# One layer of a hybrid decoder on one core: norm sums with split operands, the new tokens' matmuls placed in rows with other visits, and two down products that take their last k-tile at their end

## The chip, the cores and the metric

The kernel runs on one core of a Trainium2 chip. Its time is the device time of one execution in microseconds (us), and a kernel's time is the median of several runs. A core has a matrix engine (TensorE, PE in the profile; its weight loads are PEld), a vector engine (VectorE, DVE), an activation engine (ScalarE, ACT), a general engine (GpSimd, POOL) and a queue engine that starts most transfers (SyncE, SP). Each works through its own list of instructions in order and waits on semaphores for the others.

## The reference

One inference step of one layer for 256 prompt tokens and 8 x 4 = 32 sample tokens that share all weights (288 columns, T in the kernel), with model width 2048 and feed-forward width 5632, all in float32:

```python
z = x @ w_in                                # h, gate_b, gate_c, q, k, v, g_a, g_b
ya = gate_b * causal_dwconv3(gate_c * h)
yb = merged dilated window attention of q, k, v  (3 groups x 4 heads of 128; the sample
     tokens attend to cached keys and values and to their own new ones)
mixed = sigmoid(g_a) * (ya @ w_branch_a) + sigmoid(g_b) * (yb @ w_branch_b)
x1 = layernorm(ALPHA * x + mixed @ w_out) * ln1_g + ln1_b
a, b = split(x1 @ w_up)
y  = layernorm(ALPHA * x1 + (silu(causal_dwconv3(a)) * b) @ w_down) * ln2_g + ln2_b
```

The caches and the last rows of the convolutions are returned too.

## The kernel before

**Products.** Activations lie with the features on the 128 partitions and the 288 tokens in the columns. Each weight block is 128 output features by up to 16 k-tiles of 128. To keep float32 accuracy with the faster matmul type fp32r, both operands are split into a high part (rounded to fp32r) and a low part (the rest): `split` does it for activations, with a copy on ACT (L214) and a subtraction on DVE (L215). `prepare` (L162) loads the next weight block into `wst` (three buffers, L167) and `half_block` splits it by halves of eight k-tiles into `whi` on ACT (L138) and `wlo` on DVE (L139), four buffers each. `product` (L187) takes one prepared block, asks for the next to be prepared, and `mms` (L202) issues three matmuls for each k-tile into one PSUM accumulator `acc` (five buffers): high by high (L208), high weights by low activations (L209), low weights by high activations (L210). A full product is 48 matmuls. The program goes from one `product` to the next: q; k and v with the prompt's attention between; the convolution mixer; the gates with `w_a` and `w_b`; `w_out`; then the feed-forward part in three parts (`THIRDS`, 16, 16 and 12 tiles of 128), each with its up products (L726 and L739) and sixteen down products (L756).

**Order.** The program is written for a tile framework that adds the semaphores and orders each engine's list itself, by a model of the timeline, within the dependencies; the order written in the source is therefore not the order on an engine. `behind` and `in_a_row` (L301) force a given order on PE where they are used.

**Sample attention.** `sample_steps` (L392) is a generator that `product` advances every five or so products. A step is one visit of PE: plain float32 matmuls of 32 output rows for each head against cache tiles, tied together by `in_a_row`. Scores are L407, the values L460. The softmax lies between them (L428 to L434), then the transposes of the probabilities (L437, L439) and of the new values (L447). DVE masks the operands of a visit by batch (L369). The scores of the new tokens against each other are twelve small matmuls at L424, issued in the step after the last score visit; the new tokens' part of the values are four matmuls at L471, after the first value visit. `fetch_two` loads the next two cache tiles through SP and stores them to the output.

**Norms.** `Norm` (L600) keeps, for each of two layer norms, the running sums of the deviations and of their squares over 16 feature tiles. `first` takes the mean over partitions of the first tile as an offset with one float32 matmul against `ones_p` (L610). `add` adds each tile to the sums on POOL (L622, L623); the last tile is not added there: the sums and the last tile each go through a float32 matmul against `ones_d` (L630, L631), four in all. `finish` makes mean and 1/std for the first norm (L636), `finish_out` the end of the kernel (L650). The first norm's result is not applied before the up products of part one: they run on scaled but unnormalised tiles, and `normed` (L709) corrects each result with 1/std (L714, L715).

**Part one of the feed-forward.** Its gated tiles are split into `yah`/`yal` (here `gh`, `gl`), one k-tile after the other; the down products read all sixteen. Meanwhile POOL and ACT turn `dd` into the normalised tile (L750 to L752), which is split into `xh`/`xl` for the later parts (L758).

Of the kernel before, what the change touches and what calls it, by code (L numbers as in the profile page):

```python
# [11 lines left out]
F32R = mybir.dt.float32r  # L12
# [5 lines left out]
P = 128  # L18
# [65 lines left out]
def layer_kernel(ctx: ExitStack, tc: tile.TileContext, ins, outs):  # L84
# [14 lines left out]
    def sb(pl, shape, tag, dt=F32, bufs=None):  # L99
        return pl.tile(shape, dt, tag=tag, name=nm(tag), bufs=bufs)  # L100

    def acc(half=H):
        return sb(ps, [P, half, 2], "acc")
# [4 lines left out]
    def h3(ap):  # L108
        return ap.rearrange("p k (h a) -> p k h a", h=2)

    def att(cols=512):
        return sb(ps, [P, cols], "att", bufs=2)

    def f32(ap):
        return ap.bitcast(F32)
# [68 lines left out]
                if prompt[1] is None:  # L184
                    prompt[0] = None

    def product(x):  # L187

        w = w_ready.pop(0)
        if not w_ready:  # L190
            prepare()
        if steps_on[0]:
            spent[0] += N_STEP
            while spent[0] >= N_STEP_BLOCKS:
                spent[0] -= N_STEP_BLOCKS
                next(steps, None)
        o = acc(x[0].shape[-1])
        mms(o, w, x)
        prompt_step()
        return o.rearrange("p a h -> p h a")  # L200

    def mms(out, w, x):  # L202
        nk = sum(n for _, _, n in w)
        k = 0
        for hi, lo, n in w:
            for c in range(n):
                xh_k, xl_k = (t[:, k].rearrange("p h a -> p a h") for t in x)
                pe.matmul(out, hi[:, c, :], xh_k, start=k == 0, stop=False)  # L208
                pe.matmul(out, hi[:, c, :], xl_k, start=False, stop=False)  # L209
                last_mm[0] = pe.matmul(out, lo[:, c, :], xh_k, start=False, stop=k == nk - 1)  # L210
                k += 1

    def split(hi, lo, src):
        act.copy(hi, src)  # L214
        dve.tensor_tensor(lo, src, f32(hi), ALU.subtract)  # L215

    ones_d = sb(big, [P, P], "ones_d")
    ones_p = sb(big, [P, P], "ones_p")
    pool.memset(ones_d, 1.0 / D)
    pool.memset(ones_p, 1.0 / P)  # L220


    zero = sb(wk, [P, T], "cy", F32R, bufs=2)
# [168 lines left out]
    def sample_steps():  # L392
        fetch_two()
        yield
        row = []
        s = sw2[:, :SW]
        sbias = cst[:, C_SB : C_SB + SW]
        for g in range(NG):
            qm = by_batch(q_s[:, g])
            cols = P if g == 0 else NT * P  # L400
            p = sb(ps, [P, cols], "long", bufs=1)
            for b in range(NB):
                if g > 0 or b % 4 == 0:
                    c = cache_tiles.pop(0)
                o = (b % 4) * NH * P if g == 0 else 0
                for j in range(NH):
                    row.append(pe.matmul(  # L407
                        p[j * NS : (j + 1) * NS], qm[:, j, b, :], c[:, o + j * cols : o + (j + 1) * cols],
                        start=b == 0, stop=b == NB - 1,
                    ))  # L410
                if b == NB - 1 or (g > 0 and b % 2 == 1):
                    in_a_row(row)
                    row = []
                    fetch_two()
                    yield
            sg = s[:, g * P : (g + 1) * P]
            if g == 0:
                dve.tensor_tensor(sg, p, sbias[:, :P], ALU.add)
            else:
                pick_t(sg, p, sbias[:, g * P : (g + 1) * P])  # L420
        pn = sb(ps, [P, NG * NS], "long", bufs=1)
        for j in range(NH):
            for g in range(NG):
                pe.matmul(  # L424
                    pn[j * NS : (j + 1) * NS, g * NS : (g + 1) * NS], q_s[:, g, j, :], k_s[:, g, j, :],
                    start=True, stop=True,
                )
        dve.tensor_tensor(s[:, NG * P :], pn, sbias[:, NG * P :], ALU.add)  # L428
        st = sb(wk, [P, 4], "st", bufs=4)
        dve.reduce_max(st[:, 0:1], s, AX.X)  # L430
        dve.tensor_scalar_mul(st[:, 1:2], st[:, 0:1], -SCALE)
        act.activation(s, s, AF.Exp, bias=st[:, 1:2], scale=SCALE, accum_out=st[:, 2:3])
        dve.reciprocal(st[:, 3:4], st[:, 2:3])
        dve.tensor_scalar_mul(s, s, st[:, 3:4])  # L434
        pt = att()
        for g in range(NG):
            pe.transpose(pt[:, g * P : (g + 1) * P], s[:, g * P : (g + 1) * P], ident)  # L437
        pt2 = att()
        pe.transpose(pt2[: NG * NS, :P], s[:, NG * P :], ident)  # L439
        sT = sw2[:, : NG * P].rearrange("p (g r) -> p g r", g=NG)  # L440
        act.copy(sT, pt[:, : NG * P].rearrange("p (g r) -> p g r", g=NG))
        sTn = sw2[: NG * NS, NG * P : NG * P + P]
        act.copy(sTn, pt2[: NG * NS, :P])
        vn = sw2[: NG * NS, NG * P + P : NG * P + P + NH * P].rearrange("p (j d) -> p j d", j=NH)
        pv = att()
        for j in range(NH):
            pe.transpose(pv[: NG * NS, j * P : (j + 1) * P], v_s[:, j].rearrange("p g r -> p (g r)"), ident)  # L447
        act.copy(vn, pv[: NG * NS].rearrange("p (j d) -> p j d", j=NH))
        o_sb = sw2[:, NG * P + P + NH * P : NG * P + 2 * P + NH * P]
        for g in range(NG):  # L450
            sm = by_batch(sT[:, g].rearrange("p (j r) -> p j r", j=NH))
            cols = P if g == 0 else NT * P
            if g < 2:
                p = sb(ps, [P, cols], "long", bufs=1)
            for b in range(NB):
                if g > 0 or b % 4 == 0:
                    c = cache_tiles.pop(0)
                o = (b % 4) * NH * P if g == 0 else 0
                for j in range(NH):
                    row.append(pe.matmul(  # L460
                        p[j * NS : (j + 1) * NS], sm[:, j, b, :], c[:, o + j * cols : o + (j + 1) * cols],
                        start=b == 0 and g < 2, stop=b == NB - 1 and g == 2,
                    ))
                if b == NB - 1 or (g > 0 and b % 2 == 1):
                    in_a_row(row)
                    row = []
                    fetch_two()
                    yield
            if g == 0:
                for j in range(NH):  # L470
                    pe.matmul(  # L471
                        p[j * NS : (j + 1) * NS], sTn[:, j * NS : (j + 1) * NS], vn[:, j, :], start=False, stop=True
                    )
                act.copy(o_sb, p)
            elif g == 2:
                pick_t(o_sb, p, o_sb)
        po = att(P)
        pe.transpose(po, o_sb, ident)
        oT = sw[:, :P]
        act.copy(oT, po)  # L480
        split(ybh[:, :, SEQ:], ybl[:, :, SEQ:], oT.rearrange("p (j r) -> p j r", j=NH))
        yield
# [117 lines left out]
    class Norm:  # L600


        def __init__(self, g, b):
            self.g, self.b = g, b
            self.s1, self.s2, self.c = (lw[:, k] for k in range(3))

        def first(self):

            p = att(T)
            pe.matmul(p, ones_p, dd[:, 0], start=True, stop=True)  # L610
            act.copy(self.c, p)
            dve.tensor_tensor(dd[:, 0], dd[:, 0], self.c, ALU.subtract)

        def add(self, i):
            d = dd[:, i]
            last = i == KD - 1
            q = self.s2 if i == 0 else sb(wk, [P, T], "cy", bufs=2)
            act.activation(q, d, AF.Square)
            if i == 0:
                pool.tensor_copy(self.s1, d)  # L620
            elif not last:
                pool.tensor_tensor(self.s1, self.s1, d, ALU.add)  # L622
                pool.tensor_tensor(self.s2, self.s2, q, ALU.add)  # L623
            if i == KD - 2:

                act.activation(lw[:, 3, 0:1], q[:, 0:1], AF.Abs_reciprocal_sqrt)
            if last:
                self.p1, self.p2 = att(T), att(T)
                for p, s, e in ((self.p1, self.s1, d), (self.p2, self.s2, q)):
                    pe.matmul(p, ones_d, s, start=True, stop=False)  # L630
                    pe.matmul(p, ones_d, e, start=False, stop=True)  # L631

        def at(self, c, i):
            return prm[:, c + i : c + i + 1]
# [51 lines left out]
                sp.dma_start(out[:, k0 : k0 + n, :], y[:, k0 : k0 + n, :])  # L686


    n1 = Norm(R_LN, R_LN + KD)
    for i in range(KD):  # L690
        o = product((h3(mxh), h3(mxl)))
        xf = sb(wk, [P, T], "h", bufs=2)
# [25 lines left out]

    cf = sb(big, [P, KF, 2 + 2 * NB], "qk_s")
    f = 0  # L720
    n2 = Norm(R_LN + 2 * KD, R_LN + 3 * KD)
    for part, nf in enumerate(THIRDS):
        gh = sb(big, [P, KD, T], "yah", F32R)
        gl = sb(big, [P, KD, T], "yal", F32R)
# [27 lines left out]
                act.activation(dd[:, k], dd[:, k], AF.Identity, bias=n1.at(n1.b, k), scale=n1.at(n1.g, k))  # L752
        if f == KF:
            sp.dma_start(outs["o_cf"].rearrange("p (k r) -> p k r", k=KF), cf)
        for i in range(KD):
            o = product((h3(gh), h3(gl)))  # L756
            if part == 0:
                split(x[0][:, i], x[1][:, i], h2(dd[:, i]))  # L758
                dve.scalar_tensor_tensor(h2(dd[:, i]), h2(dd[:, i]), ALPHA, o, ALU.mult, ALU.add)
# [194 lines left out]
```

## Time and profile before

| | |
|---|---|
| median of 3 runs | 1764.37 us (1764.05 to 1764.5) |
| the profiled execution's own time | 1764.45 us |
| its span (first to last instruction of the profile) | 1762.7 us |
| busy: PE / PEld / DVE / ACT / POOL | 1744.4 / 1713.7 / 1008.0 / 797.3 / 254.1 us |
| mean granted clock of PE | 0.997 |
| DMA | 436.25 MB, mean 247 GB/s |
| matmuls of `product`, by line L208 / L209 / L210 | 4512 each, about 0.286 us from start to end of one |
| plain float32 records of the norms, L610 / L630 / L631 | 4 / 8 / 8, 0.406 us each |
| records L424 / L471 | 24 / 8, 0.200 / 0.285 us each |

A plain float32 matmul shows as two records. Matmuls are pipelined, so the time that one takes of PE is read from the distance between starts, not from its duration. A line number in the profile is a line of the kernel before, and the same work has other numbers in the changed kernel.

### The profile page before, as it was taken

To read this page: it belongs to the slowest core of one execution; us is meant where nothing else is said; L and a number is where in the kernel's file an instruction comes from. 1 tells how busy PE (TensorE), PEld (TensorE's weight loads), DVE (VectorE), ACT (ScalarE), POOL (GpSimd) and SP (SyncE) were. 2 spreads that over 40 slices of the span, in tenths; PEclk is the share of its full clock that TensorE was granted. 3 is DMA by queue.
4 is the path that set the end of the run, shared out by engine and by line. 5 is a ranking of instruction groups with operands and counts; after the bars stand their busy time and mean duration, and the time that the engine had idled before them with its cause. 6 is when DMAs were issued, how large, how long until landed. Compare 5 with 4: busy or idle time off the path is not lost.

```text
span 1762.7 us, 33587 instructions
## 1 busy us (share of the span) xinstructions
PE 1744.4 (99%) x14275; PEld 1713.7 (97%) x14275; DVE 1008.0 (57%) x1317; ACT 797.3 (45%) x1167; POOL 254.1 (14%) x401
## 2 busy tenths in 40 slices
PE   9999999999999999999999999999999999999996
PEld 9999999999999999999999999999999999999996
DVE  5444455555555444455588788774555554555564
ACT  5444444333434333344455655553444443345444
POOL 0000000000000000001155233310011110011174
PEclk9999999999999999999999999999999999999998
DMA  8477787787787887467766566656565666666653
GB/s 325 173 287 266 270 299 297 266 324 295 273 332 282 306 314 264 150 247 260 282 233 221 220 230 217 237 216 236 218 237 218 236 219 234 220 234 221 237 198 108
DMA packets 60198, 436.25 MB, mean 247 GB/s; under 512 B 7184, under 2 KB 8336, under 8 KB 16016
## 3 DMA queue, kind: packets, MB, share of 16 engines
q1 hardware_dynamic: 58320, 429.40, 66.2%
q10 hardware_dynamic: 1728, 4.72, 0.7%
q8 instruction: 111, 1.82, 0.4%
q14 instruction: 39, 0.32, 0.0%
HBM read 389.89 MB, written 94.53 MB: 275 GB/s over the span
## 4 chain that ended last, share of the span: by engine, by line
PE 97%; DMA 1%; ACT 1%; DVE 1%; POOL 0%; issue 0%; SPq 0%; ACTq 0%; DVEq 0%
PE acc L208 31%; PE acc L209 31%; PE acc L210 31%; PE long L407 1%; PE long L460 1%; DMA wst<-in_w_in 1%; PE att L348 0%; DMA dd<-in_w_in 0%; PE att L312 0%; ACT whi L138 0%; POOL qk_s L535 0%; ACT yah L685 0%; DVE dd L661 0%; ACT xh L214 0%; PE att L340 0%; PE att L332 0%
## 5 line engine op out<-in xcount | busy, mean ns | idle before, releaser
L139 DVE TENSOR_TENSOR wlo<-wst,whi 128x1024 fp32r<-128x1024 f32 (+1 forms) x580 | 711.1, 1227 | 617.8 <-ACT whi L138 610.8
L138 ACT CAST whi<-wst 128x1024 fp32r<-128x1024 f32 (+1 forms) x580 | 592.0, 1022 | 877.1 <-PE acc L209 769.5
L208 PE MATMUL acc<-xh,whi 128*128 128x288 f32 (+1 forms) x3232 | 928.0, 287 | 0.0
L210 PE MATMUL acc<-xh,wlo 128*128 128x288 f32 (+1 forms) x3232 | 925.4, 286 | 0.1
L209 PE MATMUL acc<-xl,whi 128*128 128x288 f32 (+1 forms) x3232 | 925.0, 286 | 0.0
L208 PEld LDWEIGHTS acc<-xh,whi 128*128 128x128 f32 x3232 | 610.8, 189 | 8.0 <-ACT cy L519 2.5
L210 PEld LDWEIGHTS acc<-xh,wlo 128*128 128x128 f32 x3232 | 610.8, 189 | 1.2 <-issue 0.8
L209 PEld LDWEIGHTS acc<-xl,whi 128*128 128x128 f32 x3232 | 610.9, 189 | 0.4 <-issue 0.2
L208 PE MATMUL acc<-yah,whi 128*128 128x288 f32 x1216 | 348.2, 287 | 0.3 <-ACT yah L214 0.3
L210 PE MATMUL acc<-yah,wlo 128*128 128x288 f32 x1216 | 347.8, 286 | 0.0
L209 PE MATMUL acc<-yal,whi 128*128 128x288 f32 x1216 | 347.6, 286 | 0.0
L208 PEld LDWEIGHTS acc<-yah,whi 128*128 128x128 f32 x1216 | 229.7, 189 | 3.2 <-ACT h L577 2.5
L210 PEld LDWEIGHTS acc<-yah,wlo 128*128 128x128 f32 x1216 | 229.8, 189 | 0.1
L209 PEld LDWEIGHTS acc<-yal,whi 128*128 128x128 f32 x1216 | 229.8, 189 | 0.1
L535 POOL COPY qk_s<-u 128x2 f32<-128x2 f32 x44 | 41.8, 949 | 573.7 <-ACT u L735 441.5
L521 DVE SCALAR_TENSOR_TENSOR cy<-u,prm,cy 128x304 f32<-128x304 f32 x120 | 70.7, 589 | 3.1 <-ACT cy L519 0.4
L592 POOL TENSOR_TENSOR ya<-ya,dd 128x288 f32<-128x288 f32 x16 | 13.6, 852 | 306.0 <-DVE ya L591 306.0
L546 DVE TENSOR_TENSOR ya<-cy,acc 128x144 f32<-128x144 f32 x132 | 25.6, 249 | 33.6 <-PE acc L210 33.6
L535 POOL COPY cm<-u 128x2 f32<-128x2 f32 x16 | 3.0, 187 | 254.1 <-DVE u L560 254.1
L214 ACT CAST yah<-ya 128x288 fp32r<-128x288 f32 x76 | 32.7, 431 | 14.0 <-POOL ya L592 8.8
L215 DVE TENSOR_TENSOR yal<-ya,yah 128x288 fp32r<-128x288 f32 x76 | 34.9, 459 | 1.3 <-ACT yah L214 1.2
L622 POOL TENSOR_TENSOR cache<-cache,dd 128x288 f32<-128x288 f32 x28 | 27.7, 988 | 46.6 <-DVE dd L701 31.5
(166 smaller groups left out, 812.4 us busy)
## 6 DMA issues: line engine op xcount, KB each, us to landing
wst<-in_w_in SPq DMA_DIRECT2D x114, 1024.0 KB, 6.0
wst<-in_w_up SPq DMA_DIRECT2D x88, 1024.0 KB, 4.8
wst<-in_w_down SPq DMA_DIRECT2D x32, 1024.0 KB, 4.9
cache<-in_ck SPq DMA_DIRECT2D x18, 1024.0 KB, 6.4
out_o_ck<-cache SPq DMA_DIRECT2D x18, 1024.0 KB, 9.3
cache<-in_cv SPq DMA_DIRECT2D x18, 1024.0 KB, 6.3
out_o_cv<-cache SPq DMA_DIRECT2D x18, 1024.0 KB, 9.9
wst<-in_w_a SPq DMA_DIRECT2D x16, 1024.0 KB, 4.9
```

Of the source, the lines that this page charges most:

```text
L138: act.copy(hi[:, :n, :], st[:, k0 : k0 + n, :])
L139: dve.tensor_tensor(lo[:, :n, :], st[:, k0 : k0 + n, :], f32(hi[:, :n, :]), ALU.subtract)
L208: pe.matmul(out, hi[:, c, :], xh_k, start=k == 0, stop=False)
L209: pe.matmul(out, hi[:, c, :], xl_k, start=False, stop=False)
L210: last_mm[0] = pe.matmul(out, lo[:, c, :], xh_k, start=False, stop=k == nk - 1)
L214: act.copy(hi, src)
L215: dve.tensor_tensor(lo, src, f32(hi), ALU.subtract)
L407: row.append(pe.matmul(p[j * NS : (j + 1) * NS], qm[:, j, b, :], c[:, o + j * cols : o + (j + 1) * cols], start=b == 0, stop=b == NB - 1,))
L521: dve.scalar_tensor_tensor(y, u[:, i : i + YW], prm[:, w0 + i : w0 + i + 1], y, ALU.mult, ALU.add)
L535: pool.tensor_copy(dst[:, 0:2], u[:, SEQ : SEQ + 2])
L546: dve.tensor_tensor(a, b, c, ALU.mult)
L622: pool.tensor_tensor(self.s1, self.s1, d, ALU.add)
```

## The change

Three edits in one:

- **Norm sums.** `ones_d` and `ones_p` become fp32r tiles (1/2048 and 1/128, exact in it). In `first` the tile is copied to fp32r on ACT and the mean is taken of the copy with one fp32r matmul, in both norms. For the first norm (`tail=False`) POOL adds the last tile too, ACT and DVE split both sums into high and low parts (576 columns at once), and four fp32r matmuls replace the four float32 ones. The second norm (`tail=True`) keeps its float32 matmuls.
- **New tokens.** Their twelve score matmuls are issued with the last score visit, in one row with it, with heads in the inner loop, into an `att` buffer instead of the `long` one; their four value matmuls are issued in one row with the first value visit.
- **Down products.** The first two down products of part one are issued together by `two_products`: each first over 15 k-tiles, then both over the last one.

```diff
+    def two_products(x):
+        done = []
+        for _ in range(2):
+            done.append((acc(), next_block()))
+            mms(*done[-1], x, range(KD - 1))
+        for o, w in done:
+            mms(o, w, x, range(KD - 1, KD))
+        return [o.rearrange("p a h -> p h a") for o, _ in done]
...
-    def mms(out, w, x):
+    def mms(out, w, x, which=range(KD)):
...
-    ones_d = sb(big, [P, P], "ones_d")
-    ones_p = sb(big, [P, P], "ones_p")
+    ones_d = sb(big, [P, P], "ones_d", F32R)
+    ones_p = sb(big, [P, P], "ones_p", F32R)
...
+                if g == NG - 1 and b == NB - 1:
+                    pn = att(NG * NS)
+                    row += [
+                        pe.matmul(
+                            pn[j * NS : (j + 1) * NS, k * NS : (k + 1) * NS], q_s[:, k, j, :], k_s[:, k, j, :],
+                            start=True, stop=True,
+                        )
+                        for k in range(NG) for j in range(NH)
+                    ]
...
-        pn = sb(ps, [P, NG * NS], "long", bufs=1)
-        for j in range(NH):
-            for g in range(NG):
-                pe.matmul(
-                    pn[j * NS : (j + 1) * NS, g * NS : (g + 1) * NS], q_s[:, g, j, :], k_s[:, g, j, :],
-                    start=True, stop=True,
-                )
...
+                if g == 0 and b == NB - 1:
+                    row += [
+                        pe.matmul(
+                            p[j * NS : (j + 1) * NS], sTn[:, j * NS : (j + 1) * NS], vn[:, j, :], start=False, stop=True
+                        )
+                        for j in range(NH)
+                    ]
...
-                for j in range(NH):
-                    pe.matmul(
-                        p[j * NS : (j + 1) * NS], sTn[:, j * NS : (j + 1) * NS], vn[:, j, :], start=False, stop=True
-                    )
...
+            hi = sb(wk, [P, T], "ya", F32R, bufs=2)
+            act.copy(hi, dd[:, 0])
             p = att(T)
-            pe.matmul(p, ones_p, dd[:, 0], start=True, stop=True)
+            pe.matmul(p, ones_p, hi, start=True, stop=True)
...
-            elif not last:
+            elif not last or not self.tail:
                 pool.tensor_tensor(self.s1, self.s1, d, ALU.add)
                 pool.tensor_tensor(self.s2, self.s2, q, ALU.add)
...
-                for p, s, e in ((self.p1, self.s1, d), (self.p2, self.s2, q)):
-                    pe.matmul(p, ones_d, s, start=True, stop=False)
-                    pe.matmul(p, ones_d, e, start=False, stop=True)
+                if self.tail:
+                    for p, s, e in ((self.p1, self.s1, d), (self.p2, self.s2, q)):
+                        pe.matmul(p, f32(ones_d), s, start=True, stop=False)
+                        pe.matmul(p, f32(ones_d), e, start=False, stop=True)
+                else:
+                    w = sb(wk, [P, 4, T], "cache", F32R, bufs=2)
+                    split(w[:, 0:2], w[:, 2:4], lw[:, 0:2])
+                    for k in range(4):
+                        pe.matmul((self.p1, self.p2)[k % 2], ones_d, w[:, k], start=k < 2, stop=k >= 2)
...
-    n1 = Norm(R_LN, R_LN + KD)
+    n1 = Norm(R_LN, R_LN + KD, False)
...
-    n2 = Norm(R_LN + 2 * KD, R_LN + 3 * KD)
+    n2 = Norm(R_LN + 2 * KD, R_LN + 3 * KD, True)
...
+        early = two_products((h3(gh), h3(gl))) if part == 0 else []
         for i in range(KD):
-            o = product((h3(gh), h3(gl)))
+            o = early.pop(0) if early else product((h3(gh), h3(gl)))
```

More of the change, by code (lines that the diff above doesn't have):

```diff
@@ L185, in prompt_step, with next_block @@
                     prompt[0] = None
-    def product(x):
+    def next_block():
         w = w_ready.pop(0)
@@ L191, in product @@
             prepare()
+        return w
+    def product(x):
+        w = next_block()
         if steps_on[0]:
@@ L200, in product @@
         return o.rearrange("p a h -> p h a")
-    def mms(out, w, x):
+    def two_products(x):
[7 more added lines that the diff above has]
+    def mms(out, w, x, which=range(KD)):
         nk = sum(n for _, _, n in w)
-        k = 0
+        k = -1
         for hi, lo, n in w:
             for c in range(n):
+                k += 1
+                if k not in which:
+                    continue
                 xh_k, xl_k = (t[:, k].rearrange("p h a -> p a h") for t in x)
@@ L210, in mms @@
                 last_mm[0] = pe.matmul(out, lo[:, c, :], xh_k, start=False, stop=k == nk - 1)
-                k += 1
     def split(hi, lo, src):
@@ L215, in split @@
         dve.tensor_tensor(lo, src, f32(hi), ALU.subtract)
-    ones_d = sb(big, [P, P], "ones_d")
-    ones_p = sb(big, [P, P], "ones_p")
-    pool.memset(ones_d, 1.0 / D)
-    pool.memset(ones_p, 1.0 / P)
+    ones_d = sb(big, [P, P], "ones_d", F32R)
+    ones_p = sb(big, [P, P], "ones_p", F32R)
+    pool.memset(f32(ones_d), 1.0 / D)
+    pool.memset(f32(ones_p), 1.0 / P)
     zero = sb(wk, [P, T], "cy", F32R, bufs=2)
@@ L600, in layer_kernel, with __init__ @@
     class Norm:
-        def __init__(self, g, b):
-            self.g, self.b = g, b
+        def __init__(self, g, b, tail):
+            self.g, self.b, self.tail = g, b, tail
             self.s1, self.s2, self.c = (lw[:, k] for k in range(3))
         def first(self):
+            hi = sb(wk, [P, T], "ya", F32R, bufs=2)
+            act.copy(hi, dd[:, 0])
             p = att(T)
-            pe.matmul(p, ones_p, dd[:, 0], start=True, stop=True)
+            pe.matmul(p, ones_p, hi, start=True, stop=True)
             act.copy(self.c, p)
```

## The prediction

> **What bounds the kernel now.** I read the page first, then who TensorE (PE) waits for, then PE's timeline where the change touches it, then the vector engines beside those places.
>
> ```profile
> span 1762.7 us, 33587 instructions
> ...
> PE 1744.4 (99%) x14275; PEld 1713.7 (97%) x14275; DVE 1008.0 (57%) x1317; ACT 797.3 (45%) x1167; POOL 254.1 (14%) x401
> ```
>
> ```profile
> PE acc L227 <- DVE cy L224: 1.2, 1, 1.2
> PE acc L262 <- ACT yal L214: 1.2, 2, 0.7
> PE acc L208 <- ACT yah L214: 0.3, 1, 0.3
> PE acc L262 <- ACT xh L214: 0.2, 1, 0.2
> ```
>
> PE is busy 99% of the span and waits 2.9 us in all, most of it in the first 15 us. So an edit is worth what it changes in PE's own row of instructions, plus any wait that it makes or takes away. PE's timeline gives the prices (start, duration, line):
>
> ```profile
> 964.86 0.29 PE L210 MATMUL acc<-yah,wlo 128*128 128x288 f32 x1
> 964.98 1.13 PE L630 MATMUL att<-cache,ones_d 128*128 128x288 f32 x4
> 965.74 0.50 PE L208 MATMUL acc<-xh,whi 128*128 128x290 f32 x1
> 966.07 0.29 PE L209 MATMUL acc<-xl,whi 128*128 128x290 f32 x1
> ```
>
> Durations overlap, so starts are what counts. Split (fp32r) matmuls of 288 columns start 0.122 us apart (964.86 to 964.98). The two plain-fp32 sums at L630 (four records) push the next pair of starts to 965.74 and 966.07, where 964.98 and 965.10 would have been: 0.97 us, or 0.48 a matmul, four times a split one. The edit's other two places:
>
> ```profile
> 443.76 0.29 PE L210 MATMUL acc<-xh,wlo 128*128 128x288 f32 x1
> 443.98 0.65 PE L424 MATMUL long<-qk_s 128*32 128x32 f32 x24
> 444.55 0.39 PE L208 MATMUL acc<-xh,whi 128*128 128x288 f32 x1
> 444.78 0.29 PE L209 MATMUL acc<-xl,whi 128*128 128x288 f32 x1
> ```
>
> ```profile
> 1168.61 0.29 PE L209 MATMUL acc<-yal,whi 128*128 128x288 f32 x1
> 1169.24 0.51 PE L208 MATMUL acc<-yah,whi 128*128 128x288 f32 x2 [0.35 <-ACT yah L214]
> ```
>
> L424 alone costs 444.78 - 443.76 - 2 x 0.122 = 0.78 us, of which 0.57 (443.98 to 444.55) is its own stretch and 0.20 is getting in and out: 0.10 more than a step before it, 0.11 after it. The last fence is the one wait outside the start: 1169.24 - 1168.61 - 0.12 = 0.51 us.
>
> **Norm sums as split operands.** At L630/L631 the first norm has four fp32 matmuls in three visits. By starts they cost 0.97, 0.48 (L631 from 968.05) and 0.48 (L631 from 969.39): 1.93 us. Four split matmuls cost 4 x 0.122 = 0.49. Gain 1.44 us. The mean of the first tile (L610) is one fp32 matmul in each norm; starts 879.24, 879.51, 879.84 give 0.48, the one at 1682.38 the same. As split it is 0.12: gain 0.36 twice, 0.72.
>
> What this adds lies on other engines. One ScalarE (ACT) copy of 128x288 (0.43, the L214 row) goes ahead of each L610. For the first norm, dd tile 0 is done at 876.96 and ACT stands idle from 877.5, so the copy ends by 877.9; PE comes to the matmul six places later than before, at 879.97. For the second, dd is done at 1680.10, ACT is idle until 1681.89, PE arrives at 1682.87. No wait. For the sums POOL adds the last tile to both (L622/L623, 0.80 each alone, mean 0.99), ACT copies 576 columns (between 0.43 for 288 and 1.04 for 1024, so about 0.65) and VectorE (DVE) subtracts 576 (0.45 to 1.23, about 0.75). From dd's last tile at 965.63 and its square at 966.88: POOL ends between 967.7 and 968.7, ACT by 969.3, DVE by 970.1. In the changed order PE has 47 of the 48 matmuls of the next product ahead of the sums, 964.98 + 47 x 0.1235 = 970.8. The cover is that product; without it the chain of some 4 us would be a wait.
>
> Behind the sums, 1/std comes later: its operations on ACT and DVE now stand behind two more weight conversions, and I place the first L714 at 977.3 instead of 975.14. With PE 1.44 us ahead, the vector work of part one starts some 3 us later against the matmuls. What hides it: five accumulators of 5.9 us each, and weights converted ahead. A half block's buffer is freed three halves (8.8 us) before PE needs its new content, the conversion takes 1.05 + 1.23, so 6.5 us are spare; before, ACT's conversion at 459.51 came 2.5 us late and PE did not wait. DVE is busy 40.3 of 50 us in part one, so it recovers 2.3 us in each tile of 11.85.
>
> **New tokens' matmuls in a row with visits.** Both groups go into a visit that is there anyway, so 0.20 of getting in and out is saved twice. L471 alone costs 477.69 - 476.89 - 0.245 = 0.555. Inside the row of L460, 32 matmuls of its shape take 1.88 us, 0.059 each, so four take 0.235: gain 0.32. L424's twelve are also put in another order, so that neighbours write different column groups. Bounds: unchanged stretch, 0.57, gain 0.20; the L460 price scaled to 32 columns, 12 x 0.059 / 4 = 0.18, gain 0.60. I take 0.40, nearer to neither since the trace has no 32-column row in that order: gain 0.37.
>
> The Trainium skill's "TensorEngine Tiling (Array Packing)", section "Instruction Overhead", puts some 60 cycles on every matmul, so that narrow ones gain nothing; at the 2.4 GHz of "TensorE: Matmul & The Clock Gate" that is 25 ns a record, an estimate of 0.60 us for 24, near the 0.57 measured, and by it this group would gain only 0.2 and the sum below would be 2.7. The 7 ns between starts of neighbouring L460 records speak against it here.
>
> The sample group's softmax moves from 444.7 to about 416, where DVE and ACT have room, and the transposes at L437 to the next visit, 444.3. Then L460 comes 5.5 us after them; its masked weights (L369, 1.22) need L441 (to 445.8) and end by 447.5, PE arrives at 449.9. The copy for L471 (L448) ends by 449.6, PE arrives at 451.8. SP fetches one pair of cache tiles a block earlier, and the weight load behind their store waits for the landing: at 464.30 before, 5.4 us past its turn, now about as much on the block before. Loads lead their conversion by 12.4 us (422.83 to 435.19) and land in 6.0: 6.4 spare. DVE's second L369 holds its queue until L460 is through (452), ACT's L474 likewise; each delays a conversion by about 2.5 of the 6.5 spare. Zero.
>
> **The two down products.** The wait at 1169.24 is on the last k-tile of `yah`. The first matmul on `yah` starts at 1156.36, and 101 of them start before the wait. In source order the first product would stop after 45 (15 k-tiles of 3). 101 is 45 + 45 + 11: the scheduler already held the last k-tile of both products back, past four k-tiles of the third. The changed kernel's built order has exactly this sequence there on PE, and the same on ACT, DVE, POOL and SP. The edit moves nothing: gain 0, and the 0.51 stays.
>
> **Sum:** 1.44 + 0.72 + 0.32 + 0.37 + 0 = 2.85 us. The profiled execution took 1764.45 (span 1762.7 and 1.8 around it), 0.08 over the median of 1764.37, so 1761.6 for it and 1761.5 for the median: 0.16% less. What a measurement of this kernel can tell from no change is about 0.2%, 3.5 us; the gain is just inside it.
>
> **Rivals.** *The sums wait for POOL.* One POOL operation shows how far it can be held:
>
> ```profile
> L535 POOL COPY qk_s<-u x16: 827/832/4423, 977.4 to 1157.0; 128x2 f32<-128x2 f32 x16
> ```
>
> (minimum, median, maximum in ns.) The long one lies beside a run of DVE subtractions from 1157.25 to 1161.4. If an add for the last tile is held as long, 3.6 us, the split sums are ready at 972.9 to 973.7 and PE waits 2.1 to 2.9: 1763.6 to 1764.4. Against it: DVE has only L139 and L703 there, to 967.8, then waits itself. The Trainium skill ("SBUF — State Buffer", "SBUF: two separate sides") says that the pair of ports that both engines share is locked for a whole instruction and the other fully blocks; by that, an add waits for one DVE instruction, at most 1.3 us, and the sum stands. The row shows a hold over a whole run of them.
>
> *Part one never recovers (slower).* The late 1/std shifts part one's vector work by 3 us, 6.6 with a held POOL add; if it lasted to the end, the wait at 1169.24 would grow by it: 1764.5 or 1768.1. It decides from 2.85 us still missing after sixteen tiles. Against it: 2.3 us recovered per tile.
>
> *More comes out than the prices say.* The wait at 1169.24 follows from that 4.42 us POOL copy (ACT waits 3.74 us at L752 for it); a shift against DVE's run could free it, 0.51, and L424 may reach its low end, 0.23: 1760.8 to 1761.0, or 3.6 us gained, past 0.2%, with both.
>
> *The third edit does act*, contrary to the order: with the wait gone 1761.0; with the third product's second half converted late (freed only 3.3 us ahead, 2.3 + contention needed) about 1 us lost, 1762.5.
>
> **Numbers.** Forecast 0.66 (1761.0 to 1762.1); sums waiting 0.11; part one late 0.05; more than priced 0.15; third edit acting 0.03. The range 1760.4 to 1763.2 covers the first, most of "more" and of the third edit, and small waits at the sums. Faster by over 0.2% (below 1760.84) takes most of the "more" case and a little for gains unseen: 0.16. Slower by over 0.2% (above 1767.9) needs part one late with a held add, or a wait nobody priced: 0.04. The rest, 0.80, is within.
>
> **What would show it.** PE's timeline: sums as four starts 0.12 apart with no wait ahead of them; one record at each mean; the new tokens' rows inside the last L407 and first L460 visits, with no step of 0.22 between; about 101 `yah` matmuls, then again a wait near 0.5. PE's waits: nothing new over 0.3 us. Wrong would be: a wait of PE at the sums or for `whi`/`wlo`, a `yah` wait other than 0.3 to 0.7, or a time outside the range with PE's rows as forecast.

## The result, and the profile after

The changed kernel takes 1761.85 us (median of 22 runs, 1761.69 to 1762.24) against 1764.07 (22 runs, 1763.84 to 1764.5): 2.2 us less, a ratio of 0.9988 with a 95% interval of 0.9982 to 0.9993. That is inside what was called no change (0.2%, 3.5 us) and in the forecast's direction, 0.35 us above the forecast time. The profiled execution took 1761.81.

The page's first lines, and who PE waited for (in us: total, times, longest):

```profile
span 1760.0 us, 33583 instructions
...
PE 1741.6 (99%) x14269; PEld 1712.1 (97%) x14269; DVE 1008.0 (57%) x1318; ACT 798.2 (45%) x1170; POOL 254.1 (14%) x403
```

```profile
PE acc L244 <- DVE cy L241: 1.2, 1, 1.2
PE acc L279 <- ACT xh L231: 0.6, 2, 0.4
PE acc L228 <- DVE wlo L139: 0.6, 1, 0.6
PE acc L226 <- ACT yah L231: 0.3, 1, 0.3
PE acc L279 <- ACT yal L231: 0.3, 1, 0.3
```

The waits of the start are of the same kind and shift by tenths from run to run; the `yah` wait is unchanged. One line is new: PE waits for the low part of a weight block (`wlo`, L139). PE's timeline of the changed kernel at the four places (start, duration; lines have new numbers: L664 the sums, L432 the new scores, L226 to L228 the three split matmuls):

```profile
968.92 0.29 PE L227 MATMUL acc<-xl,whi 128*128 128x290 f32 x1
969.04 0.42 PE L664 MATMUL att<-cache,ones_d 128*128 128x288 f32 x2
969.30 0.29 PE L228 MATMUL acc<-xh,wlo 128*128 128x290 f32 x1
...
412.06 1.92 PE L424 MATMUL long<-cache,sw 128*32 128x512 f32 x16
413.80 0.37 PE L432 MATMUL att<-qk_s 128*32 128x32 f32 x24
414.10 0.39 PE L226 MATMUL acc<-xh,whi 128*128 128x288 f32 x1
...
1165.46 0.29 PE L227 MATMUL acc<-yal,whi 128*128 128x288 f32 x1
1166.09 0.39 PE L226 MATMUL acc<-yah,whi 128*128 128x288 f32 x1 [0.35 <-ACT yah L231]
...
1702.39 0.29 PE L227 MATMUL acc<-yal,whi 128*128 128x288 f32 x1
1703.28 0.39 PE L228 MATMUL acc<-yah,wlo 128*128 128x288 f32 x1 [0.60 <-DVE wlo L139]
1703.50 0.29 PE L226 MATMUL acc<-yah,whi 128*128 128x288 f32 x1
```

Two sum matmuls now take 969.30 - 969.04 = 0.26 us. The twelve score matmuls sit right behind the visit's last cache matmuls: from their first start to the next split matmul are 0.30 us (413.80 to 414.10). The same visit before, without them:

```profile
412.31 0.29 PE L210 MATMUL acc<-xh,wlo 128*128 128x288 f32 x1
412.53 1.92 PE L407 MATMUL long<-cache,sw 128*32 128x512 f32 x16
414.38 0.39 PE L208 MATMUL acc<-xh,whi 128*128 128x288 f32 x1
414.61 0.29 PE L209 MATMUL acc<-xl,whi 128*128 128x288 f32 x1
```

That visit costs 414.61 - 412.31 - 2 x 0.122 = 2.06 us, and 2.24 with the scores in it (414.32 - 411.84 - 2 x 0.122): they add 0.18. The `yah` wait is 1166.09 - 1165.46 - 0.12 = 0.51, as before. The new wait is 1703.28 - 1702.39 - 0.12 = 0.77, and the next start comes 0.10 late too: 0.87 in all.

By starts, before less after:

| place | forecast gain, us | measured gain, us |
|---|---|---|
| first norm's sums, 1.94 to 0.53 | 1.44 | 1.41 |
| two means, 0.485 to 0.135 and 0.138 | 0.72 | 0.70 |
| new tokens' scores with the last score visit, 2.82 to 2.24 | 0.37 | 0.58 |
| new tokens' values with the first value visit, 2.64 to 2.30 | 0.32 | 0.33 |
| down products | 0 | 0 |
| wait for `wlo` in the second norm | 0 | -0.87 |
| sum | 2.85 | 2.15 |

The sum agrees with the medians' 2.22. The two spans differ by 2.7 because the profile of before also lost some 0.5 us more in its first microseconds (its first cache matmul starts at 129.00, after's at 128.52); in the twelve profiles of this case that start lies between 128.46 and 129.00, and the kernels below called tokens_only (128.48) and heads_outer (128.92) show that it does not go with the edits.

The new wait stands where ACT squares the second norm's tiles. Before, then after (start, duration, and in brackets the idle time before and what ended it):

```profile
1695.60 1.05 ACT L138 CAST whi<-wst 128x1024 fp32r<-128x1024 f32 x1 [2.31 <-PE acc L209]
1700.34 0.44 ACT L618 ACTIVATE cy<-dd 128x288 f32<-128x288 f32 x1 [3.69 <-POOL cache L623]
1700.69 0.60 ACT L138 CAST whi<-wst 128x512 fp32r<-128x512 f32 x1
1703.05 0.44 ACT L618 ACTIVATE cy<-dd 128x288 f32<-128x288 f32 x1 [1.76 <-POOL cache L623]
```

```profile
1693.53 0.62 ACT L138 CAST whi<-wst 128x512 fp32r<-128x512 f32 x1 [0.38 <-PE acc L227]
1698.39 0.44 ACT L645 ACTIVATE cy<-dd 128x288 f32<-128x288 f32 x1 [4.25 <-POOL cache L650]
1699.90 0.44 ACT L645 ACTIVATE cy<-dd 128x288 f32<-128x288 f32 x1 [1.06 <-POOL cache L650]
1700.25 1.03 ACT L138 CAST whi<-wst 128x1024 fp32r<-128x1024 f32 x1
```

A square needs one of two `cy` buffers, and POOL frees them with its sums (L650, before L623), which stand behind a run of subtractions (L796, before L762). POOL before, then after:

```profile
1683.54 15.64 POOL L762 TENSOR_TENSOR dd<-dd,cache 128x288 f32<-128x288 f32 x14 [13.41 <-ACT cache L611]
1699.13 0.42 POOL L620 COPY cache<-dd 128x288 f32<-128x288 f32 x1
1699.52 0.79 POOL L623 TENSOR_TENSOR cache<-cache,cy 128x288 f32<-128x288 f32 x1
```

```profile
1680.53 15.96 POOL L796 TENSOR_TENSOR dd<-dd,cache 128x288 f32<-128x288 f32 x14 [13.55 <-ACT cache L638]
1696.43 0.42 POOL L647 COPY cache<-dd 128x288 f32<-128x288 f32 x1
1696.81 0.80 POOL L796 TENSOR_TENSOR dd<-dd,cache 128x288 f32<-128x288 f32 x1
1697.57 0.79 POOL L650 TENSOR_TENSOR cache<-cache,cy 128x288 f32<-128x288 f32 x1
```

Before, one such square stood ahead of the next weight conversion (L138). After, two do, and one more subtraction stands ahead of the first sum. So the conversion starts 6.1 us after the one before it ended (1694.15 to 1700.25), DVE's half of it ends at 1703.2, and PE wanted it at 1702.5.

### The profile page after: what moved, and what is told of

Its sections match the earlier page's. It is cut to its first block, busy times and chain, and to the rows that moved or that the text cites. A ratio compares the mean times of both kernels' runs of the same rounds, so it can differ in the third digit from the quotient of the medians.

```text
span 1760.0 us, 33583 instructions
## 1 busy us (share of the span) xinstructions
PE 1741.6 (99%) x14269; PEld 1712.1 (97%) x14269; DVE 1008.0 (57%) x1318; ACT 798.2 (45%) x1170; POOL 254.1 (14%) x403
## 4 chain that ended last, share of the span: by engine, by line
PE 96%; POOL 1%; ACT 1%; DMA 1%; DVE 1%; issue 0%; SPq 0%; ACTq 0%; DVEq 0%
PE acc L226 31%; PE acc L228 31%; PE acc L227 31%; PE long L424 1%; PE long L480 1%; POOL dd L796 1%; DMA wst<-in_w_in 0%; PE att L365 0%; DMA dd<-in_w_in 0%; PE att L329 0%; ACT whi L138 0%; POOL qk_s L559 0%; DVE wlo L139 0%; ACT yah L718 0%; DVE dd L694 0%
## 5 line engine op out<-in xcount | busy, mean ns | idle before, releaser
L139 DVE TENSOR_TENSOR wlo<-wst,whi 128x1024 fp32r<-128x1024 f32 (+1 forms) x580 | 709.5, 1224 | 619.4 <-ACT whi L138 615.2
L138 ACT CAST whi<-wst 128x1024 fp32r<-128x1024 f32 (+1 forms) x580 | 592.1, 1022 | 869.8 <-PE acc L227 760.2
L226 PE MATMUL acc<-xh,whi 128*128 128x288 f32 (+1 forms) x3232 | 927.6, 287 | 0.0
L228 PE MATMUL acc<-xh,wlo 128*128 128x288 f32 (+1 forms) x3232 | 925.0, 286 | 0.1
L226 PEld LDWEIGHTS acc<-xh,whi 128*128 128x128 f32 x3232 | 610.8, 189 | 7.7 <-ACT h L579 2.5
L228 PEld LDWEIGHTS acc<-xh,wlo 128*128 128x128 f32 x3232 | 610.8, 189 | 0.3 <-DVE wlo L139 0.3
L226 PE MATMUL acc<-yah,whi 128*128 128x288 f32 x1216 | 348.0, 286 | 0.3 <-ACT yah L231 0.3
L228 PE MATMUL acc<-yah,wlo 128*128 128x288 f32 x1216 | 347.7, 286 | 0.6 <-DVE wlo L139 0.6
L226 PEld LDWEIGHTS acc<-yah,whi 128*128 128x128 f32 x1216 | 229.7, 189 | 3.1 <-ACT h L601 2.5
L228 PEld LDWEIGHTS acc<-yah,wlo 128*128 128x128 f32 x1216 | 229.8, 189 | 0.8 <-DVE wlo L139 0.8
```

Source lines behind the costliest of these rows:

```text
L138: act.copy(hi[:, :n, :], st[:, k0 : k0 + n, :])
L139: dve.tensor_tensor(lo[:, :n, :], st[:, k0 : k0 + n, :], f32(hi[:, :n, :]), ALU.subtract)
```

## The experiments

Every kernel was timed in alternation with the kernel before, whose medians lay between 1763.97 and 1764.03. Differences are against the median of before of the same comparison. The 95% interval of a ratio to before reaches about 0.0009 (1.5 us) to either side in these comparisons, so by it alone norm_only and tokens_only cannot be told apart from before. The runs of each kernel lie closer together than that (within 0.8 us, source_order's within 1.4), no run of a changed kernel overlaps with a run of before, and the parts are read from PE's starts.

**One edit at a time.** norm_only is before with the norm edit alone. Shown is what it takes out of the changed kernel; the lines of before come back in their place.

```diff
-                if g == NG - 1 and b == NB - 1:
-                    pn = att(NG * NS)
-                    row += [...]
...
-                if g == 0 and b == NB - 1:
-                    row += [...]
...
-        early = two_products((h3(gh), h3(gl))) if part == 0 else []
...
```

> The kernel before with the norm edit alone (split sums in the first norm, split mean in both). Theory A (prices by PE's starts, and a weight conversion that comes late in the second norm because ACT's list is ordered otherwise there): the sums give 1.42 us and the means 0.70, the late conversion takes back 0.86, so 1.25 us less than before, with a PE wait for wlo of 0.6 to 0.9 us some 23 us after the second norm's mean. Rival B (the wait has to do with the tokens or the down products): 2.1 us less, no such wait.

Measured: 1762.72, 1.31 less than before; its profile has the `wlo` wait (0.76 us from 1703.35, counted as above) and the `yah` wait. So the wait belongs to the norm edit.

tokens_only is before with the new tokens' matmuls in the two rows; the lines that this replaces are left out here.

```diff
+                if g == NG - 1 and b == NB - 1:
+                    pn = att(NG * NS)
+                    row += [...]
...
+                if g == 0 and b == NB - 1:
+                    row += [...]
...
```

> The kernel before with the new tokens' matmuls in the two rows, nothing else. Theory A: 0.59 us from the twelve score matmuls and 0.33 from the four value matmuls, 0.92 us less than before, and no PE wait for wlo in the second norm. Rival B: part of the after kernel's gain there is timing of the start (its profile begins 0.48 us earlier), then about 0.4 us less.

Measured: 1763.02, 1.01 less, and no `wlo` wait. The two parts add up to 2.32; the changed kernel has 2.22.

no_down is the changed kernel without the third edit.

```diff
-        early = two_products((h3(gh), h3(gl))) if part == 0 else []
         for i in range(KD):
-            o = early.pop(0) if early else product((h3(gh), h3(gl)))
+            o = product((h3(gh), h3(gl)))
```

> The changed kernel without the third edit (the first two down products are issued one after the other again). Theory A (the scheduler had already held both last k-tiles back): the same as the changed kernel, 2.2 us less than before, the yah wait of 0.51 us where it was. Rival B (the edit does act, through the order in which the next blocks are prepared): different from the changed kernel by 0.4 us or more, or another yah wait.

Measured: 1761.71, 2.32 less than before; both waits are where they were (0.51 from 1165.39, 0.78 from 1702.32). The third edit is worth nothing that can be measured.

**What holding back is worth.** source_order takes the holding back away from the scheduler: each of the first three down products of part one runs through all its k-tiles in order.

```diff
-                pe.matmul(out, hi[:, c, :], xh_k, start=k == 0, stop=False)
-                pe.matmul(out, hi[:, c, :], xl_k, start=False, stop=False)
+                three = [
+                    pe.matmul(out, hi[:, c, :], xh_k, start=k == 0, stop=False),
+                    pe.matmul(out, hi[:, c, :], xl_k, start=False, stop=False),
+                ]
+                before = last_mm[0]
                 last_mm[0] = pe.matmul(out, lo[:, c, :], xh_k, start=False, stop=k == nk - 1)
+                if chain[0]:
+                    in_a_row([before, *three, last_mm[0]])
...
+            chain[0] = part == 0 and i < 3
...
```

> The changed kernel with the first three down products of part one held on PE in plain order: all 16 k-tiles of one before the next, no last k-tile held back. Theory A (the scheduler's own holding back was already worth what the third edit is meant to bring): PE waits for yah and yal after 45 matmuls instead of 101, 7.4 us for yah less 0.5 to 1 that ACT gains, then about 1.2 for yal, so 1768 to 1770. Rival B (without the matmuls in between the vector engines come earlier, and little is lost): under 1764.

Measured: 1770.94, 7.0 more than before and 9.1 more than the changed kernel (ratio to before 1.0039, 1.0027 to 1.0052). Its profile:

```profile
1165.97 0.61 PE L228 MATMUL acc<-yah,whi 128*128 128x288 f32 x1 [7.07 <-ACT yah L237]
1166.47 0.61 PE L229 MATMUL acc<-yal,whi 128*128 128x288 f32 x1
1166.87 0.45 PE L232 MATMUL acc<-yah,wlo 128*128 128x288 f32 x1
```

PE stood from 1158.62 to 1165.97, 7.2 us longer than a start distance, and came back slow: starts are 0.24 us apart until 1171.90, and the granted clock reads 0.50 from 1166 to 1169. From 1165.97 to 1171.90 are 23 distances between starts in 5.93 us, where 0.1225 each would be 2.8: 3.1 us more, 2.7 of it for the distance of 0.24 and 0.4 in the first two distances (0.50 and 0.40), where the second matmul reads `yal`. The profiled execution took 1771.62, 9.8 more than that of the changed kernel, and 7.2 + 3.1 - 0.5 (the `yah` wait that it replaces) is that. Theory A had the wait for `yah` about right (7.2 for 6.4 to 6.9). Of the 1.2 that it put on `yal` at most 0.4 shows, and it had no slow stretch, which is why the median lies above its range. The Trainium skill ("TensorE: Matmul & The Clock Gate", "Part 1") says that PE falls to half clock after an idle window of about 3.4 us; the 7.2 us here did it, the waits under 1 us did not (the granted clock of the changed kernel reads 1.00 from 1166 to 1168 and from 1703 to 1705). Where between the two the limit lies, no run here shows.

**Where the new wait comes from.** mean2_fp32 gives the second norm its plain float32 mean back.

```diff
-            hi = sb(wk, [P, T], "ya", F32R, bufs=2)
-            act.copy(hi, dd[:, 0])
             p = att(T)
-            pe.matmul(p, ones_p, hi, start=True, stop=True)
+            if self.tail:
+                pe.matmul(p, f32(ones_p), dd[:, 0], start=True, stop=True)
+            else:
+                hi = sb(wk, [P, T], "ya", F32R, bufs=2)
+                act.copy(hi, dd[:, 0])
+                pe.matmul(p, ones_p, hi, start=True, stop=True)
```

> The changed kernel, but the second norm's mean of the first tile is a plain float32 matmul again, without the ACT copy ahead of it. Theory A (the copy moved ACT's and POOL's lists there, and with that came the late conversion): PE pays 0.35 us more for the mean and loses the wlo wait, 0.86: 0.5 us faster than the changed kernel, 2.7 us less than before. Rival B (the wait comes from the shift in time against the transfers, whatever the lists): 0.35 us slower than the changed kernel, 1.85 less than before, with the wait still there.

Measured: 1761.31, 2.72 less than before, 0.5 less than the changed kernel. No `wlo` wait in its profile, and ACT's list has one square ahead of the conversion again, as before (it waits 3.68 us for POOL, and L138 starts at 1697.62). So the split mean of the second norm, worth 0.35 on PE, cost 0.87 through the order of the lists.

more_square_buffers gives the squares six buffers by using three tags in turn.

```diff
-            q = self.s2 if i == 0 else sb(wk, [P, T], "cy", bufs=2)
+            q = self.s2 if i == 0 else sb(wk, [P, T], ("cy", "ya", "h")[i % 3] if self.tail else "cy", bufs=2)
```

> The changed kernel; the squares of the second norm take turns in six buffers instead of two. Theory A (ACT's squares wait for POOL to free one of two buffers, and the weight conversions behind them come late): the ACT wait of 4.25 us ahead of the square goes, so does PE's wlo wait, 0.86: 1761.0, 3.0 less than before. Rival B (the conversions are late because of their place behind the squares, which then wait for the tile from POOL and DVE itself, not for a buffer): the wlo wait stays at 0.3 or more, 1761.5 to 1761.9.

Measured: 1761.05, 2.92 less than before. ACT's timeline there:

```profile
1693.55 0.62 ACT L138 CAST whi<-wst 128x512 fp32r<-128x512 f32 x1 [0.43 <-PE acc L227]
1694.99 0.44 ACT L645 ACTIVATE ya<-dd 128x288 f32<-128x288 f32 x1 [0.82 <-DVE dd L797]
1696.48 1.04 ACT L138 CAST whi<-wst 128x1024 fp32r<-128x1024 f32 x1 [1.05 <-PE acc L227]
```

The square comes 3.4 us earlier and waits for its tile, not for POOL; the conversion behind it starts at 1696.48 instead of 1700.25. PE has no `wlo` wait left.

paced_subtracts attacks the other end: POOL's subtractions no longer run ahead of its sums.

```diff
-                pool.tensor_copy(self.s1, d)
+                self.added = [pool.tensor_copy(self.s1, d)]
...
-                pool.tensor_tensor(self.s2, self.s2, q, ALU.add)
+                self.added.append(pool.tensor_tensor(self.s2, self.s2, q, ALU.add))
...
-                    pool.tensor_tensor(dd[:, i], dd[:, i], n2.c, ALU.subtract)
+                    i_sub = pool.tensor_tensor(dd[:, i], dd[:, i], n2.c, ALU.subtract)
+                    if i > 4:
+                        behind(i_sub, n2.added[i - 4])
```

> The changed kernel; POOL takes the subtraction of the offset from tile i only behind the sums of tile i-4, where it ran the subtractions of all fifteen ahead of nearly all sums. Theory A (POOL's thirteen to fourteen subtractions in front of the first sums of squares keep ACT's buffers): the buffers come free in step, PE's wlo wait goes, 1761.0. Rival B (then tiles reach DVE later, and DVE's conversions stand behind them): wlo waits in other places, 1762 or more.

Measured: 1761.07, 2.90 less than before, no `wlo` wait. ACT's list here:

```profile
1695.16 0.45 ACT L645 ACTIVATE cy<-dd 128x288 f32<-128x288 f32 x1 [0.66 <-DVE dd L799]
1696.81 1.05 ACT L138 CAST whi<-wst 128x1024 fp32r<-128x1024 f32 x1 [1.20 <-PE acc L227]
```

The square waits for its tile and not for POOL, with two buffers as in the changed kernel. Both ends of the chain from POOL's run over the buffers to the conversion cure it: the cause is shown.

**The old wait.** last_norm_later queues ACT's normalisation of part one's last tile behind the last copy to `yah`.

```diff
-        act.copy(hi, src)
+        i = act.copy(hi, src)
...
+        return i
...
-            split(gh[:, k], gl[:, k], gf)
+            i_y = split(gh[:, k], gl[:, k], gf)
...
-                act.activation(dd[:, k], dd[:, k], AF.Identity, bias=n1.at(n1.b, k), scale=n1.at(n1.g, k))
+                i_n = act.activation(dd[:, k], dd[:, k], AF.Identity, bias=n1.at(n1.b, k), scale=n1.at(n1.g, k))
+                if k == nf - 1:
+                    behind(i_n, i_y)
```

> The changed kernel; on ACT the normalisation of part one's last tile is queued behind the copy that makes the last k-tile of yah. Theory A (the yah wait comes from ACT standing 3.7 us at that normalisation for POOL, whose small copy is held for 4.4 us): the wait of 0.51 goes, 1761.35, 2.7 less than before. Rival B (yah is as late for DVE's sake): the wait stays, 1761.8.

Measured: 1761.31, 2.66 less than before.

```profile
1163.40 0.43 ACT L231 CAST yah<-ya 128x288 fp32r<-128x288 f32 x1
```

The last `yah` copy starts at 1163.40 instead of 1165.61 and PE's `yah` wait is gone; POOL's small copy is still held for 4.42 us, but ACT no longer stands behind it.

**The order of the heads.** heads_outer keeps the twelve score matmuls in the row, in the old order.

```diff
-                        for k in range(NG) for j in range(NH)
+                        for j in range(NH) for k in range(NG)
```

> The changed kernel with the twelve new score matmuls in the old order inside the row (heads in the outer loop, so that three neighbours write the same 32 columns of the array). Theory A (neighbours in different column groups overlap, and that gave 0.38 us): the row with them costs 2.62 instead of 2.24 us, 0.38 more than the changed kernel, 1762.2. Rival B (only the saved visit matters, each matmul costs its issue): no difference, 1761.85.

Measured: 1762.06, 1.93 less than before.

```profile
414.19 0.62 PE L432 MATMUL att<-qk_s 128*32 128x32 f32 x24
414.75 0.39 PE L226 MATMUL acc<-xh,whi 128*128 128x288 f32 x1
```

The row costs 2.49 us by starts against 2.24: the order is worth 0.25, the saved visit the other 0.33. Between A and B, nearer A. The trace also has each record's own start: the 24 starts lie over 0.42 us here, 18.5 ns apart on average, and over 0.175 us in the changed kernel, 7.6 apart; the way back to the split matmuls takes another 0.13 in both.

**Both cures.** both_fixes is more_square_buffers and last_norm_later together.

> The changed kernel with six buffers for the second norm's squares and with the last tile's normalisation queued behind the last copy of yah: the two cures together. Theory A (the two waits are independent): 0.86 and 0.51 us less than the changed kernel, 1760.5, 3.5 less than before, and no wait of PE after the first 15 us. Rival B (curing one moves the lists at the other place): between 1761.0 and 1761.8.

Measured: 1760.48 (1760.22 to 1760.94), 3.51 less than before, ratio 0.9981 (0.9972 to 0.9989): faster than both kernels. After the first 15 us PE waits for nothing in its profile.

## Why the prediction was right, and where not

**The norms' terms** were right: 1.41 for 1.44 and 0.70 for 0.72. For work of which the trace of before has a row, prices by the distance of starts hold to 0.03. The cover held as well: PE reached the sums at 969.04 with DVE's half of the split done at 968.08; POOL's two adds took 0.80 and 1.30. The "sums wait for POOL" rival did not happen, nor did "part one never recovers": the first correction by 1/std (L747) came at 975.36, and the last tile of `dd` ended 1.74 us earlier than before (963.89 for 965.63), so on the clock of before that is 977.1, against the 977.3 I placed it at. The vector work of part one did start that late against the matmuls, and sixteen tiles later the `yah` wait was the same 0.51: it had recovered.

**The new tokens' values** were right. **The scores** were mis-sized: 0.58 for 0.37, at the low end of the bounds (0.60). What failed here is the choice "nearer to neither". The row of L460, 7 ns between starts of neighbours in different column groups, was the row to take: the 24 records start 7.6 ns apart on average and add 0.18 us, its scaled price, where I took 0.40. The Trainium skill's 60 cycles a matmul ("TensorEngine Tiling (Array Packing)", "Instruction Overhead"), by my estimate 25 ns, does not hold for them in this order. In the old order most starts lie 26 to 32 ns apart, near it, with some of 1 to 6 between them, so that the average of 18.5 is below it there too.

**The down products** were right: 0, with 101 matmuls read from the trace as the reason, and source_order shows that the holding back was there and worth 9.1 us.

**The step that failed outright** is "For the second, dd is done at 1680.10, ACT is idle until 1681.89 ... No wait." It looked for a wait at the matmul behind the copy, and there was none. It did not follow ACT's and POOL's lists further: the built order of the changed kernel, which I used for the down products, shows there that a square moved ahead of a conversion, and one POOL subtraction ahead of a sum. The trace of before had ACT idle 3.69 us for POOL at that square; a conversion queued behind two of them had a price that could have been bounded. It was 0.87 us, 30% of the forecast gain. Its place among the rivals was only the remainder "a wait nobody priced", and it is one of the prediction's own signs of being wrong: a wait of PE for `wlo`, 0.60 us in PE's list of waits, where nothing new over 0.3 was to come. Of the "more comes out" rival the smaller part came, the scores (0.21 of 0.23); the larger, the `yah` wait, stayed, as forecast, with the POOL copy behind it held 4.43 us again (maximum; median 0.83).

**What was luck.** The time was 0.35 us off, the gain 0.63 (2.85 forecast, 2.22 measured). Two things that the prediction did not see made the time look better than its account: the scores gave 0.21 more and so hid a part of the 0.87, and the three runs of before from which the forecast time was counted (1764.37) lay 0.3 above the median of the later 22 (1764.07).

## What to carry to other kernels

When one engine is busy 99% of the time, its edits can be priced to a few hundredths of a microsecond by the distance of starts, where the trace already has work of the same shape in the same order; what remains open is the order of the other engines' lists, so compare these lists over the whole program, not only beside the edit. A source edit that asks for an order does nothing where the scheduler already made it: count instructions in the trace between the first use and the wait. An engine that stands in order behind a buffer which a slower engine frees is a place to look first: four buffers more, or subtractions less far ahead, gave 0.7 us on top of the changed kernel's gain, twice what the split mean that stumbled there was worth on PE (0.35).

## What the runs showed of the hardware

Narrow plain float32 matmuls (32 columns of the array, 32 moving columns) started 7.6 ns a record apart on average when neighbours went to different column groups and 18.5 when three matmuls in a row went to the same one. A wait of 7.2 us brought PE back at a granted clock of 0.50 for about 6 us, at a price of 2.7 us on top of the wait. POOL's 128x2 copy beside a run of DVE subtractions took 4.4 us in all twelve profiles, against a median of 0.83: in the changed kernel it ended at 1158.31, when DVE's run did (1158.26). That this run is what held it is read from the times; no run here takes it away. The Trainium skill's lock for one instruction ("SBUF — State Buffer", "SBUF: two separate sides") does not by itself give that length.
